# Final scaling in six pieces, extra sums on the Pool engine, and all low halves on DVE

## The chip, the cores and the metric

The kernel runs on one core of one Trainium2 chip, in float32 from end to end. The metric is the device time of one execution in microseconds, as the median of several runs. A profile of one such execution shows every instruction of the five engines: PE (TensorE, with its weight loads as PEld), DVE (VectorE), ACT (ScalarE), POOL (GpSimd) and SP (SyncE, which issues most DMAs).

## The reference, cut to what matters

One decoder layer over 256 tokens: a SwiGLU feed-forward block, a mixer, a second SwiGLU block, and a last RMS norm. The change lies in the second block and in the last norm.

```python
def rmsnorm(x, g):
    y = x32 * lax.rsqrt(jnp.mean(x32 * x32, axis=-1, keepdims=True) + EPS) * g
def swiglu(x, w_gate, w_up, w_down):
    return (jax.nn.silu(x @ w_gate) * (x @ w_up)) @ w_down
h = h + 0.5 * swiglu(rmsnorm(h, ffn2_norm[l]), ffn2_w_gate[l], ffn2_w_up[l], ffn2_w_down[l])
return rmsnorm(h, final_norm)
```

D_MODEL is 2048 and D_FF is 5504. The 256 tokens lie on 128 partitions in two blocks, tb = 0 and 1.

## The kernel before, in words

**A product in three passes.** To keep float32 accuracy, each operand is split into a high half and a low half, and each product is made of three matmuls (`mm3`, lines 95 to 97): high by high, high by low, low by high. The activations' halves (xh, xl) are made once and kept; the weights' halves are made as they stream in. `product` (line 99) walks along the contraction in steps of 4 blocks of 128 rows: `wraw` (line 69) loads 4 blocks by one DMA on the SP queue, then `halves` (line 83) splits them, two blocks at a time, into tiles `whi` and `wlo` of 128x1024. ACT writes `whi` (line 89), and one subtraction writes `wlo` (line 90), as a rule on DVE. Twelve matmuls (two blocks, two token blocks, three passes) consume such a pair. I call it a half and count the halves of the down product's first column chunk from 0 to 21. `whi` and `wlo` have four buffers each, `wraw` three, so ACT and DVE work at most four halves ahead of PE.

**The feed-forward block.** `ffn` (line 295) makes gate and up products for 11 column chunks. DVE then turns each chunk's result with 32 small transposes (line 170, in `turn_split`), which stand in DVE's queue between the subtractions, and `gT` collects 11 pairs of halves. Then come four down products (c = 0 to 3), each 43 blocks deep and 512 columns wide, that is 22 halves, and after each `finish(c)`: in the second block that is `last_chunk` (line 981). It squares and sums h on ACT for the last norm and, for c under 3, multiplies h by its gain (`gfin`, loaded in the call for c = 0 by the ACT queue, line 987). In the product for c = 1 four of the low halves are subtracted on POOL instead of DVE (argument `pooled`, lines 90, 118 and 326).

**The end.** The product for c = 3 holds back the last blocks of token block 1 (`tail`), so that token block 0 finishes some 4 us earlier. For each token block `ffn2` then makes the norm's factor r (lines 968 on DVE and 969 on POOL) and scales the four column chunks: chunk 3 on DVE (line 974, with the gain), chunk 1 on DVE (line 976), chunks 0 and 2 on ACT (line 978), each followed by its output DMA (line 979), from SP for odd chunks and from ACT for even ones.

**What sets the order.** A planner puts each engine's instructions into a queue at build time. It takes what is ready first, as well as the order of the source; each engine then works its queue strictly in order and waits on semaphores. Tiles of up to 4 KB per partition share a ring of 32 slots (`slot`, line 57): a new tile waits until the last reader of its slot's previous tile is done.

Of the kernel before, what the change touches and what calls it, by code (L numbers as in the profile page):

```python
# [9 lines left out]
F32 = mybir.dt.float32  # L10
# [6 lines left out]
P = 128  # L17
D_MODEL = 2048
SEQ = 256
D_FF = 5504  # L20
# [11 lines left out]
class Layer:  # L32
# [47 lines left out]
            k += m  # L80
        return raw

    def halves(self, raw, pool=False):

        nc = self.nc
        _, nk, n = raw.shape
        hi = self.wpool.tile([P, 2, 512], F32R, tag="whi", bufs=4, name=self.name("whi"))
        lo = self.wpool.tile([P, 2, 512], F32R, tag="wlo", bufs=4, name=self.name("wlo"))
        nc.scalar.activation(hi[:, :nk, :n], raw, AF.Copy)  # L89
        (nc.gpsimd if pool else nc.vector).tensor_sub(lo[:, :nk, :n], raw, hi[:, :nk, :n].bitcast(F32))  # L90
        return hi, lo

    def mm3(self, out, xh, xl, wh, wl, first, last):
# [2 lines left out]
        nc.tensor.matmul(out, xh, wl, start=False, stop=False)  # L96
        nc.tensor.matmul(out, xl, wh, start=False, stop=last)  # L97

    def product(self, accs, xT, w, r0, nkt, c0, n, tail=0, pooled=()):


        held = []
        for k0 in range(0, nkt, 4):
            nk = min(4, nkt - k0)
            opening = self.fetch is not None and self.xraw is not None and k0 == 0
            raw = self.wraw(w, r0 + k0 * P, nk, c0, n, (1, 1, 2) if opening else (4,))
            if self.fetch is not None:
                self.fetch(k0 // 4 + 1)
            while any(x is xT[k0 // 4] for x, _ in self.turns):
                self.turns.popleft()[1]()  # L110
            xh, xl = xT[k0 // 4]
            for kk, ke in ((0, 1), (1, 2), (2, 4)) if opening else ((0, 2), (2, 4)):
                ke = min(ke, nk)
                if kk >= ke:
                    continue
                if self.fetch is not None:
                    self.split_x(k0 + kk, k0 + ke)
                wh, wl = self.halves(raw[:, kk:ke, :n], k0 in pooled and kk == 2)
                for k in range(kk, ke):
                    for tb in range(NTB):  # L120
                        ts = slice(tb * P, (tb + 1) * P)
                        mm = partial(
                            self.mm3, accs[tb][:, :n], xh[:, k, ts], xl[:, k, ts], wh[:, k - kk, :n],
                            wl[:, k - kk, :n], k0 + k == 0, k0 + k == nkt - 1,
                        )
                        if tb and k0 + 4 * tail >= nkt:
                            held.append(mm)
                        else:
                            mm()
                while self.soon and k0 + kk >= 2:  # L130
                    self.soon.popleft()()
                for _ in range(min(3, len(self.turns))):
                    self.turns.popleft()[1]()
                self.step()
        for mm in held:
            mm()
# [158 lines left out]
    def ffn(self, wg, wu, wd, finish, tail=0):  # L295
        nc = self.nc
        gT = []
        for c0, n in FCH:
            G = [self.acc("g") for _ in range(NTB)]
            with self.tc.manual_schedule() if self.fetch is not None else nullcontext():  # L300
                self.product(G, self.xT, wg, 0, 16, c0, n)
            self.xraw = None
            U = [self.acc("u") for _ in range(NTB)]
            self.product(U, self.xT, wu, 0, 16, c0, n)
            if self.fetch is not None:
                self.fetch = None
                self.norms()
            pair = self.pair()
            gT.append(pair)
            src = [self.tmp([P, 512], "silu", 2) for _ in range(NTB)]  # L310
            for tb, s in enumerate(src):
                nc.scalar.activation(s[:, :n], G[tb][:, :n], AF.Silu, scale=self.r[tb])
                nc.vector.scalar_tensor_tensor(
                    s[:, :n], U[tb][:, :n], self.r[tb], s[:, :n], op0=ALU.mult, op1=ALU.mult
                )
            if self.later:
                for tb, s in enumerate(src):
                    self.soon.append(partial(self.transpose_split, pair, s, tb, n // P))
            else:
                self.turn_split(pair, src, n // P)  # L320
        self.xT = [None] * 4
        self.st = self.stat(4)
        for c in range(4):
            Y = [self.acc("y") for _ in range(NTB)]
            self.product(Y, gT, wd, 0, D_FF // P, c * 512, 512, tail if c == 3 else 0,
                         (8, 16, 24, 32) if tail and c == 1 else ())
            for tb in range(NTB):
                hs = self.h[:, tb, c * 512 : (c + 1) * 512]
                nc.vector.scalar_tensor_tensor(hs, Y[tb], 0.5, hs, op0=ALU.mult, op1=ALU.add)
            finish(c)  # L330
# [219 lines left out]
    def ssm_groups(self):  # L550
# [3 lines left out]
        for ct in range(8):  # L554
# [14 lines left out]
            def powered(mre, mim, k0, signs):  # L569


                tt = self.slot([P, 4, 256], s="tt")

                def product(t, power, m):
                    for r in range(2):
                        bs = slice(4 * ct + 2 * r, 4 * ct + 2 * r + 2)
                        v.tensor_mul(
                            tt[:, t, r * P : (r + 1) * P].rearrange("s (j x h) -> s x j h", j=4, x=2),
                            self.pw[:, power, k0 : k0 + 4, bs].rearrange("s k b -> s b k").unsqueeze(3)
                            .to_broadcast([P, 2, 4, 16]),  # L580
                            m[:, 2 * r : 2 * r + 2].unsqueeze(2).to_broadcast([P, 2, 4, 16]),
                        )

                product(0, 0, mre)
                product(1, 1, mim)
                v.tensor_tensor(tt[:, 0], tt[:, 0], tt[:, 1], op=signs[0])
                yield tt
                product(2, 0, mim)
                product(3, 1, mre)
                v.tensor_tensor(tt[:, 2], tt[:, 2], tt[:, 3], op=signs[1])  # L590
                yield tt
# [369 lines left out]
    def ffn2(self):  # L961
        t, nc = self.t, self.nc
        self.gfin = None
        self.ffn(t["ffn2_w_gate"][0], t["ffn2_w_up"][0], t["ffn2_w_down"][0], self.last_chunk, 2)
        out = self.out
        for tb in range(NTB):
            r = self.tmp([P, 1], "rstd", 6)
            nc.vector.tensor_scalar(r, self.st[tb][:, 3:4], 1.0 / D_MODEL, self.part[tb], op0=ALU.mult, op1=ALU.add)
            nc.gpsimd.tensor_tensor(r, r, self.mhalf, op=ALU.pow)
            for c in (3, 0, 1, 2):  # L970
                cs = slice(c * 512, (c + 1) * 512)
                hs = self.h[:, tb, cs]
                if c == 3:
                    nc.vector.scalar_tensor_tensor(hs, hs, r, self.gfin[c], op0=ALU.mult, op1=ALU.mult)
                elif c == 1:
                    nc.vector.tensor_scalar(hs, hs, r, None, op0=ALU.mult)
                else:
                    nc.scalar.activation(hs, hs, AF.Copy, scale=r)
                (nc.sync if c % 2 else nc.scalar).dma_start(out[tb, :, cs], hs)

    def last_chunk(self, c):
        nc = self.nc
        if self.gfin is None:
            gf = self.t["final_norm"].rearrange("(o d) -> o d", o=1)
            self.gfin = [self.slot([P, 512], s="gfin") for _ in range(4)]
            for i in range(4):
                nc.scalar.dma_start(
                    self.gfin[i], gf[:, i * 512 : (i + 1) * 512].broadcast_to([P, 512])
                )
        for tb in range(NTB):  # L990
            hs = self.h[:, tb, c * 512 : (c + 1) * 512]
            self.square(self.st[tb], c, hs, 512)
            if c < 3:
                nc.vector.tensor_mul(hs, hs, self.gfin[c])
        if c == 2:
            self.part = []
            for tb in range(NTB):
                p = self.tmp([P, 1], "rstd", 6)
                nc.vector.tensor_reduce(p, self.st[tb][:, :3], axis=mybir.AxisListType.X, op=ALU.add)
                nc.vector.tensor_scalar(p, p, 1.0 / D_MODEL, EPS, op0=ALU.mult, op1=ALU.add)  # L1000
                self.part.append(p)
# [67 lines left out]
```

## Time and profile before

| What | us |
|---|---|
| median of 3 runs | 1809.5 |
| lowest and highest run | 1808.77 and 1809.67 |
| the profiled execution's own time | 1809.42 |
| span of its profile | 1807.6 |
| PE busy within the span | 1792.1 |
| DVE, ACT and POOL busy | 1174.1, 859.3 and 99.9 |

The span is what the engines' records cover; 1.8 us of the execution lie outside it. A line of the timeline reads: start and length in us, engine and line of the kernel, operation, output <- inputs, shape, count, and in brackets the idle time before it and what ended it. Times within the span count from its start.

### The profile page before, as it was taken

The numbers are of one execution on the slowest core, as the hardware profiler recorded it, in microseconds if no ns is written. First come the engines' busy times: TensorE is split into PE (matmuls) and PEld (weight loads), VectorE is DVE, ScalarE is ACT, GpSimd is POOL, SyncE is SP. The second block draws the span as 40 slices with busy tenths as digits, with TensorE's granted clock in tenths as the row PEclk, the third lists the DMA queues.
The fourth block names the chain that finished last, engine by engine and source line by source line (L and its number), as shares of the span: only waits on it lengthen the run. The fifth ranks groups of instructions, "written<-read, shape, count | busy, mean of one in ns | idle before, by whom it ended". The sixth has DMA issues, their size and how long they took to land.

```text
span 1807.6 us, 22050 instructions
## 1 busy us (share of the span) xinstructions
PE 1792.1 (99%) x8365; PEld 1502.2 (83%) x8365; DVE 1174.1 (65%) x2024; ACT 859.3 (48%) x1190; POOL 99.9 (6%) x177
## 2 busy tenths in 40 slices
PE   8999999999999999999999999999999999999997
PEld 6888888788988888888888888888888888988886
DVE  5796588777765545566766565776777777853453
ACT  6544567444444434443358555444444444443443
POOL 2102022500000000000000000000000000002000
PEclk9999999999999999999999999999999999999999
DMA  8667667865555557676443455556556555665553
GB/s 321 198 218 242 202 233 255 266 218 181 190 191 201 181 192 267 202 272 239 155 147 133 140 186 186 187 192 201 189 189 201 192 187 163 212 224 191 199 197 117
DMA packets 180330, 364.18 MB, mean 201 GB/s; under 512 B 8256, under 2 KB 17344, under 8 KB 179968
## 3 DMA queue, kind: packets, MB, share of 16 engines
q1 hardware_dynamic: 172192, 343.96, 56.7%
q0 software_dynamic: 6736, 16.69, 2.7%
q10 hardware_dynamic: 1296, 2.13, 0.4%
q8 instruction: 65, 1.06, 0.2%
q14 instruction: 41, 0.34, 0.1%
HBM read 346.36 MB, written 16.38 MB: 201 GB/s over the span
## 4 chain that ended last, share of the span: by engine, by line
PE 93%; DVE 3%; DMA 1%; issue 1%; ACT 1%; POOL 0%; SPq 0%; POOLq 0%; ACTq 0%
PE y L96 9%; PE y L95 9%; PE y L97 9%; PE u L96 8%; PE u L97 8%; PE u L95 8%; PE g L96 7%; PE g L97 7%; PE g L95 7%; PE pr L95 3%; PE pr L97 3%; PE pr L96 3%; PE wo L95 2%; PE wo L97 2%; PE wo L96 2%; DVE turned L170 1%
## 5 line engine op out<-in xcount | busy, mean ns | idle before, releaser
L90 DVE TENSOR_TENSOR wlo<-wraw,whi 128x1024 fp32r<-128x1024 f32 (+2 forms) x629 | 752.1, 1201 | 551.2 <-ACT whi L89 548.4
L89 ACT ACTIVATE whi<-wraw 128x1024 fp32r<-128x1024 f32 (+2 forms) x633 | 657.2, 1042 | 771.5 <-PE y L97 247.3
L95 PE MATMUL g<-whi,xh 128*128 128x512 f32 (+1 forms) x704 | 271.7, 386 | 2.2 <-ACT whi L89 2.1
L96 PE MATMUL g<-wlo,xh 128*128 128x512 f32 (+1 forms) x704 | 271.1, 385 | 2.6 <-DVE wlo L90 2.6
L96 PE MATMUL u<-wlo,xh 128*128 128x512 f32 (+1 forms) x704 | 270.8, 385 | 0.1
L95 PE MATMUL u<-whi,xh 128*128 128x512 f32 (+1 forms) x704 | 270.8, 385 | 0.0
L97 PE MATMUL g<-whi,xl 128*128 128x512 f32 (+1 forms) x704 | 270.6, 384 | 0.0
L97 PE MATMUL u<-whi,xl 128*128 128x512 f32 (+1 forms) x704 | 270.4, 384 | 0.0
L95 PE MATMUL y<-whi,xh 128*128 128x512 f32 x688 | 267.9, 389 | 0.0
L97 PE MATMUL y<-whi,xl 128*128 128x512 f32 x688 | 267.7, 389 | 0.0
L96 PE MATMUL y<-wlo,xh 128*128 128x512 f32 x688 | 267.7, 389 | 0.0
L170 DVE STREAM_TRANSPOSE turned<-silu 32x128 f32<-32x128 f32 (+1 forms) x512 | 152.8, 298 | 8.1
L96 PEld LDWEIGHTS g<-wlo,xh 128*128 128x128 f32 x704 | 132.2, 188 | 29.3 <-DVE wlo L90 4.7
L95 PEld LDWEIGHTS g<-whi,xh 128*128 128x128 f32 x704 | 132.2, 188 | 28.2 <-ACT whi L89 3.5
L96 PEld LDWEIGHTS u<-wlo,xh 128*128 128x128 f32 x704 | 132.1, 188 | 26.0 <-DVE wlo L90 1.1
L97 PEld LDWEIGHTS u<-whi,xl 128*128 128x128 f32 x704 | 132.1, 188 | 25.0
L97 PEld LDWEIGHTS g<-whi,xl 128*128 128x128 f32 x704 | 132.1, 188 | 24.9
L95 PEld LDWEIGHTS u<-whi,xh 128*128 128x128 f32 x704 | 132.1, 188 | 24.8
L97 PEld LDWEIGHTS y<-whi,xl 128*128 128x128 f32 x688 | 129.1, 188 | 26.9
L95 PEld LDWEIGHTS y<-whi,xh 128*128 128x128 f32 x688 | 129.1, 188 | 26.8
L96 PEld LDWEIGHTS y<-wlo,xh 128*128 128x128 f32 x688 | 129.1, 188 | 26.6
L95 PE MATMUL pr<-whi,xh 128*128 128x512 f32 x256 | 101.9, 398 | 0.0
(212 smaller groups left out, 1515.7 us busy)
## 6 DMA issues: line engine op xcount, KB each, us to landing
wraw<-in_ffn_w_up SPq DMA_DIRECT2D x80, 1024.0 KB, 5.1
wraw<-in_ffn_w_down SPq DMA_DIRECT2D x80, 1024.0 KB, 5.1
wraw<-in_ffn_w_gate SPq DMA_DIRECT2D x79, 1024.0 KB, 5.1
wraw<-in_w_in SPq DMA_DIRECT2D x32, 1024.0 KB, 5.4
wraw<-in_w_out SPq DMA_DIRECT2D x16, 1024.0 KB, 5.1
wraw<-in_ffn_w_gate SPq DMA_DIRECT2D x8, 768.0 KB, 4.5
wraw<-in_ffn_w_up SPq DMA_DIRECT2D x8, 768.0 KB, 4.5
wraw<-in_ffn_w_down SPq DMA_DIRECT2D x8, 768.0 KB, 4.4
```

What stands on the lines that cost most here:

```text
L89: nc.scalar.activation(hi[:, :nk, :n], raw, AF.Copy)
L90: (nc.gpsimd if pool else nc.vector).tensor_sub(lo[:, :nk, :n], raw, hi[:, :nk, :n].bitcast(F32))
L95: nc.tensor.matmul(out, xh, wh, start=first, stop=False)
L96: nc.tensor.matmul(out, xh, wl, start=False, stop=False)
L97: nc.tensor.matmul(out, xl, wh, start=False, stop=last)
L170: nc.vector.transpose(raw[32 * b : 32 * b + 32, :nt, tb * P + 32 * a : tb * P + 32 * a + 32], src[tb][32 * a : 32 * a + 32, : nt * P].rear ...
```

## The change

The diff does three things. It takes the `pooled` choice away, so that every low half is subtracted on DVE. It adds, in the call of `last_chunk` for c = 0, three slot tiles of 128x1024, two memsets and sixteen equal additions of two of them into the third on POOL, whose result nobody reads. And at the end it scales in the order chunk 1 (DVE), two parts of chunk 0 (ACT), chunk 3 (DVE), two parts of chunk 2 (ACT), with all six output DMAs of a token block issued by SP.

```diff
-    def halves(self, raw, pool=False):
+    def halves(self, raw):
...
-        (nc.gpsimd if pool else nc.vector).tensor_sub(lo[:, :nk, :n], raw, hi[:, :nk, :n].bitcast(F32))
+        nc.vector.tensor_sub(lo[:, :nk, :n], raw, hi[:, :nk, :n].bitcast(F32))
...
-                wh, wl = self.halves(raw[:, kk:ke, :n], k0 in pooled and kk == 2)
+                wh, wl = self.halves(raw[:, kk:ke, :n])
...
-            self.product(Y, gT, wd, 0, D_FF // P, c * 512, 512, tail if c == 3 else 0,
-                         (8, 16, 24, 32) if tail and c == 1 else ())
+            self.product(Y, gT, wd, 0, D_FF // P, c * 512, 512, tail if c == 3 else 0)
...
-            for c in (3, 0, 1, 2):
-                cs = slice(c * 512, (c + 1) * 512)
+            pieces = ((1, 0, 512), (0, 0, 256), (0, 256, 512), (3, 0, 512), (2, 0, 256), (2, 256, 512))
+            for c, lo, up in pieces:
+                cs = slice(c * 512 + lo, c * 512 + up)
...
-                (nc.sync if c % 2 else nc.scalar).dma_start(out[tb, :, cs], hs)
+                nc.sync.dma_start(out[tb, :, cs], hs)
...
+        if c == 0:
+
+            z = [self.slot([P, 1024], s="z") for _ in range(3)]
+            for x in z[:2]:
+                nc.gpsimd.memset(x, 0.0)
+            for _ in range(16):
+                nc.gpsimd.tensor_add(z[2], z[0], z[1])
```

## Rows read from the trace of the kernel before

**Rows 1.** The page, parts 1 and 4: busy time by engine, and the chain by engine.

```profile
PE 1792.1 (99%) x8365; PEld 1502.2 (83%) x8365; DVE 1174.1 (65%) x2024; ACT 859.3 (48%) x1190; POOL 99.9 (6%) x177
...
PE 93%; DVE 3%; DMA 1%; issue 1%; ACT 1%; POOL 0%; SPq 0%; POOLq 0%; ACTq 0%
```

**Rows 2.** Busy time by stage: stretch, its length, busy us (and instructions) by engine, PE clock, DMA.

```profile
1565.00:1585.00 20.00, 20.00 (x89) 16.52 (x89) 18.88 (x43) 8.66 (x9) 0.00 (x0) 1.00 0.59 199
1622.00:1681.00 59.00, 59.00 (x262) 48.87 (x261) 23.94 (x23) 24.78 (x27) 9.60 (x4) 1.00 0.56 192
```

**Rows 3.** Timeline of PE: first matmuls of the last up product and the first down product.

```profile
1547.23 0.34 PE L95 MATMUL u<-whi,xh 128*128 128x384 f32 x1
...
1564.35 0.39 PE L95 MATMUL y<-whi,xh 128*128 128x512 f32 x1
```

**Rows 4.** Timeline of DVE across the start of the first down product, 1561 to 1600.

```profile
1561.48 1.23 DVE L90 TENSOR_TENSOR wlo<-wraw,whi 128x1024 fp32r<-128x1024 f32 x1 [0.85 <-ACT whi L89]
...
1565.24 0.61 DVE L313 SCALAR_TENSOR_TENSOR silu<-u,rstd,silu 128x384 f32<-128x384 f32 x1
1565.76 2.52 DVE L170 STREAM_TRANSPOSE turned<-silu 32x96 f32<-32x96 f32 x9
1568.31 1.23 DVE L90 TENSOR_TENSOR wlo<-wraw,whi 128x1024 fp32r<-128x1024 f32 x1
...
1574.96 2.81 DVE L170 STREAM_TRANSPOSE turned<-silu 32x96 f32<-32x96 f32 x10
1577.80 1.23 DVE L90 TENSOR_TENSOR wlo<-wraw,whi 128x1024 fp32r<-128x1024 f32 x1
...
1581.08 0.95 DVE L177 TENSOR_TENSOR xl<-turned,xh 128x768 fp32r<-128x768 f32 x1
...
1595.61 1.23 DVE L90 TENSOR_TENSOR wlo<-wraw,whi 128x1024 fp32r<-128x1024 f32 x1 [1.49 <-ACT whi L89]
```

**Rows 5.** Timeline of POOL from 1300 on: the first of its four subtractions.

```profile
1629.65 2.39 POOL L90 TENSOR_TENSOR wlo<-wraw,whi 128x1024 fp32r<-128x1024 f32 x1 [530.67 <-ACT whi L89]
```

**Rows 6.** Timeline of ACT and its DMA issues: the gain loads of line 987.

```profile
1579.93 0.85 ACT L176 ACTIVATE xh<-turned 128x768 fp32r<-128x768 f32 x1 [3.40 <-DVE turned L170]
1579.94 0.82 ACTq L987 DMA_DIRECT2D gfin<-in_final_norm  x2
```

**Rows 7.** POOL's instructions by line: memsets of 128x1024.

```profile
L597 POOL MEMSET C<- x8: 972/976/987, 153.0 to 305.4; 128x1024 f32 x8
```

**Rows 8.** Timelines of DVE and POOL at 972, and of POOL at 42.

```profile
972.06 1.22 DVE L90 TENSOR_TENSOR wlo<-wraw,whi 128x1024 fp32r<-128x1024 f32 x1
...
972.22 1.46 POOL L199 TENSOR_TENSOR rstd<-rstd,even 128x1 f32<-128x1 f32 x1 [2.83 <-DVE rstd L198]
...
42.47 1.09 POOL L199 TENSOR_TENSOR rstd<-rstd,even 128x1 f32<-128x1 f32 x2 [29.70 <-DVE rstd L198]
```

**Rows 9.** Timeline of the end: scaling and output DMAs of token block 1.

```profile
1800.87 1.33 ACT L978 ACTIVATE h<-h,rstd 128x512 f32<-128x512 f32 x2 [0.91 <-POOL rstd L969]
1800.87 0.75 DVE L974 SCALAR_TENSOR_TENSOR h<-h,rstd,gfin 128x512 f32<-128x512 f32 x1 [0.67 <-POOL rstd L969]
1801.54 0.48 DVE L976 TENSOR_SCALAR h<-h,rstd 128x512 f32<-128x512 f32 x1
1801.62 0.95 ACTq L979 DMA_DIRECT2D out<-h  x2
```

**Rows 10.** Issues of the output DMAs on SP: ns shortest/median/longest.

```profile
L979 SPq DMA_DIRECT2D out<-h x4: 332/367/448, 1796.9 to 1802.1; - x4
```

**Rows 11.** Busy time in stretches of 1 us at the end; columns as in rows 2.

```profile
1799.00:1800.00 1.00, 0.00 (x0) 0.00 (x0) 0.21 (x2) 0.72 (x2) 0.00 (x0) 1.00 1.01 385
...
1802.00:1803.00 1.00, 0.00 (x0) 0.00 (x0) 0.02 (x1) 0.21 (x1) 0.00 (x0) 0.50 0.51 197
...
1804.00:1805.00 1.00, 0.00 (x0) 0.00 (x0) 0.00 (x0) 0.00 (x0) 0.00 (x0) 0.50 1.03 383
1805.00:1806.00 1.00, 0.00 (x0) 0.00 (x0) 0.00 (x0) 0.00 (x0) 0.00 (x0) 0.50 0.30 107
```

More of the change, by code (lines that the diff above doesn't have):

```diff
@@ L97, in mm3, with product @@
         nc.tensor.matmul(out, xl, wh, start=False, stop=last)
-    def product(self, accs, xT, w, r0, nkt, c0, n, tail=0, pooled=()):
+    def product(self, accs, xT, w, r0, nkt, c0, n, tail=0):
         held = []
```

## The prediction, made before the changed kernel was run

> **What bounds the kernel now.** I read the chain of waits first: PE makes 93% of it, POOL nothing, and POOL is busy 6% of the span [rows 1]. The busy time by stage then says how much room the other engines have. In the second down product (c = 1, 59 us) PE is full and DVE works 23.94 us; in the 20 us at the start of the first one PE is also full, but DVE works 18.88 us [rows 2]. So nothing that DVE or ACT does costs time as long as PE's next low half is there, and the one place where this could fail soon is 1565 to 1585, where the 32 small transposes stand between the subtractions in DVE's queue.
>
> How much room there is, the two timelines tell together. PE starts the first down product at 1564.35 [rows 3] and spends 2.72 us on a half (in steady state a subtraction every 1.23 + 1.49 us, paced by PE [rows 4]). Half n therefore starts at 1564.35 + 2.72n, and its low half is wanted 0.23 us later (a twelfth of 2.72), at the second matmul. Half 6 is wanted at 1580.9; its subtraction is the one at 1577.80, done at 1579.03 [rows 4]: 1.9 us to spare. In steady state it is more: the buffer is freed three halves (8.16 us) ahead and ACT and DVE need some 2.6 us of that, which leaves about 5.5 us.
>
> **The low halves back on DVE.** Four subtractions of 2.39 us leave POOL [rows 5] and four of 1.23 us [rows 4] come to DVE: 4.9 us in a stage where DVE idles 35 of 59 us [rows 2]. The idle time hides them; PE doesn't wait there now. Price 0, and none without that cover either, since 1.23 us is sooner than 2.39.
>
> **The sums: where they run.** The source puts them after the first down product, but POOL's queue holds nothing that keeps them there: POOL idles 530.67 us up to its first subtraction at 1629.65 [rows 5]. The gain loads of the same call show how far such work is pulled ahead: they are issued at 1579.94, some 42 us before that product ends at 1564.35 + 21 x 2.72 + 1.36 = 1622.8, and stand behind an ACT instruction that waited 3.40 us [rows 6]. On POOL only the slots can hold the sums. Of 32 slots gT keeps 22 and the gains take 4, so three of the remaining six serve: those of the second block's x halves, which come free one after the other while the last up product (1547.23 to 1564.35 [rows 3]) reads them. The gains come first and take the earliest ones. My estimate: the second memset starts when three quarters of that product are done, 1560.1, takes 0.98 us [rows 7], and the first addition starts at 1561.1. The bounds are 1556 and 1582.0, the end of the last split at L177 [rows 4].
>
> **The sums: what one costs.** No row has such an addition; the nearest is POOL's subtraction of the same shape, with two SBUF inputs too: 2.39 us [rows 5]. All four stood beside an idle DVE. What happens beside a working one shows in one place: the small power on POOL takes 0.55 us when it is alone (1.09 for two), and took 1.46 us where it started at 972.22, 0.16 us behind a DVE subtraction (972.06 to 973.28); it ended 0.40 us after that one [rows 8]. So it had 0.15 us of its start behind it, and then stood still until DVE was done: POOL's reads and a DVE subtraction exclude each other. That DVE stands still for POOL in the same way no row shows. I take it to be mutual. An addition then holds DVE's subtractions for 2.39 - 0.15 = 2.25 us; the bounds are 2.0 (if all but the 0.15 us of the power's 0.55 is a fixed cost free of reads, 2.39 - 0.40) and 2.4.
>
> [...]
>
> **The sum.** If the two engines take turns, one addition, one subtraction, a turn takes 2.25 + 1.23 = 3.48 us, against the 2.72 us in which PE eats a half. In two places two additions run with no subtraction between them: under the last product's scaling and the 9 transposes (to 1568.31) and under the 10 transposes (2.81 us) [rows 4]. The 16 additions then hold 14 DVE instructions between and behind them: halves 1 to 13 and the split at L177. The last is done at 1561.1 + 16 x 2.25 + 13 x 1.23 + 0.95 = 1614.0. PE wants half 13 at 1564.35 + 13 x 2.72 + 0.23 = 1599.9: 14.1 us late. After that DVE is quick again, and nothing is won back, since PE has no slack to win. With 2.0 us per addition it is 10.1, with 2.4 16.5; a handing over of 0.1 us per turn would add 1.4. The starting point counts little, because an earlier or later start meets the same turns: from 1582, 16 additions and the subtractions of halves 8 to 23 (half 21 a short one, some 0.7 us) end at 1637.2, where half 23 is wanted at 1622.8 + 2.72 + 0.23 = 1625.8, so 11.4 us.
>
> PE would pause for up to some 3 us at a time. [...]
>
> **The end.** After the last matmul the chain runs through the norm's factor to ACT's scaling, the output DMAs, and their transfer: 1 MB from 1802.5 (share 0.51 of that microsecond) to 1805.3 (share 0.30) at about 383 GB/s [rows 11]. Before, the first piece is out at 1801.62 (DVE's 0.75 us from 1800.87, and ACT's first issue then) [rows 9]. With chunk 1 first, DVE needs 0.48 us: 1801.35, so the stream starts 0.27 us sooner. Six issues on SP at 0.33 to 0.45 us [rows 10] put the last one at 1801.4 + 5 x 0.45 = 1803.6 at the latest; ACT's four parts, by 1.33 us for two wholes [rows 9] between 1.33 and 2.67 us in all, end by 1803.5 too. From issue to data is 0.9 us and 128 KB take 0.34 us: 1804.9, while the bus alone needs until 1802.2 + 2.75 = 1805.0. So -0.3 us; bounds -0.4 and +0.6, the latter if the issues and parts take their longest and don't overlap. SP has no other work left there; ACT loses two issues. The same DMAs of token block 0 lie 4 us earlier, beside matmuls.
>
> Forecast: 1809.42 + 14.1 - 0.3 = 1823.2 us for an execution like the profiled one; the median lies 0.1 above it, so 1823. Own range 1819 to 1830 (2.0 us per addition; 2.4 with handing over and 3 us of clock).
>
> **Rivals.** [...]
>
> Second, POOL doesn't let go between additions. DVE's half 1 (1561.48 [rows 4]) then waits for all sixteen, 1561.1 + 38.2 = 1599.3, and PE, which wants it at 1567.3, is 33 us late at least; the transposes that pile up add some 2: 1845. Against it: the pair of powers took exactly twice one [rows 8], so a start of some 0.15 us or more lies between POOL's instructions. [...]
>
> Third, on the other side: only POOL gives way, and DVE's subtractions never wait, or for under 0.3 us each, which the 1.9 us to spare absorbs over the seven halves at the start. Then the sums are free and only the end counts: 1809.1. For it: the one row that shows the conflict has POOL as the loser. It decides as soon as a subtraction's wait for an addition stays below that 0.3 us.
>
> [...]
>
> **How the numbers follow.** Forecast 0.42, first rival 0.20, second 0.08, third 0.28, something else 0.02. A measurement of this kernel tells about 0.2% (3.6 us) from no change. The third rival is "same", as is the lower third of the first (0.06, up to 1813.1); the second and the rest of the first are slower: slower 0.64, same 0.34, faster 0.02. The range takes in the third rival, the first and the forecast: 1808.5 to 1830; it leaves out the second.
>
> **What would show it.** POOL's 16 additions from about 1561, each of 2.4 to 3.7 us in the record; DVE's subtractions there longer than 1.23 us or starting late, with POOL named as what they wait for or an unexplained gap; PE idle at `wlo` between 1573 and 1615 for 14 us in all; the spacing of PE's halves near 3.5 us in that stretch. [...] Six SP issues per token block and a transfer that ends 0.3 us sooner behind the last matmul would bear out the end. What would make me wrong most easily is the direction of the wait.

## The result and the profile after

The changed kernel takes 1822.37 us (median of 6 runs, 1820.31 to 1823.99) against 1809.68 us for the kernel before (6 runs): a ratio of 1.007, 95% interval 1.006 to 1.0081. It is 12.7 us slower; the forecast was 1823. The profiled execution took 1823.05 us, its span is 1821.2 us. One execution below, of the kernel without the sums, took 2589.65 us at a mean granted clock of 0.652; the ratios leave it out.

The page of the changed kernel, parts 1 and 4, answers to [rows 1]:

```profile
PE 1798.3 (99%) x8365; PEld 1504.7 (83%) x8365; DVE 1203.2 (66%) x2028; ACT 860.1 (47%) x1194; POOL 141.3 (8%) x191
...
PE 75%; DVE 5%; issue 2%; ACT 1%; DMA 1%; POOL 0%; POOLq 0%; ACTq 0%
```

POOL is 41 us busier, yet the chain still gives POOL nothing: what it costs shows under other names. Here is POOL's timeline, from 1300 on, for the changed kernel (start, length, engine, line, operation, count, idle time before):

```profile
1557.00 0.95 POOL L994 MEMSET z<- 128x1024 f32 x1 [457.30 <-PE u L97]
1561.03 0.95 POOL L994 MEMSET z<- 128x1024 f32 x1 [3.08 <-ACT whi L89]
1562.07 50.38 POOL L996 TENSOR_TENSOR z<-z,z 128x1024 f32<-128x1024 f32 x16
```

Its first two additions by themselves:

```profile
1562.07 2.40 POOL L996 TENSOR_TENSOR z<-z,z 128x1024 f32<-128x1024 f32 x1
1564.54 3.26 POOL L996 TENSOR_TENSOR z<-z,z 128x1024 f32<-128x1024 f32 x1
```

The sums begin at 1562.07, before the product that they follow in the source has begun. The first addition, ahead of DVE, takes 2.40 us; the sixteen last 50.38 us. Beside them runs DVE (its timeline; it answers to [rows 4]):

```profile
1562.22 3.32 DVE L90 TENSOR_TENSOR wlo<-wraw,whi 128x1024 fp32r<-128x1024 f32 x1 [0.85 <-ACT whi L89]
...
1565.47 3.42 DVE L90 TENSOR_TENSOR wlo<-wraw,whi 128x1024 fp32r<-128x1024 f32 x1
...
1569.86 2.51 DVE L170 STREAM_TRANSPOSE turned<-silu 32x96 f32<-32x96 f32 x9
1572.41 2.29 DVE L90 TENSOR_TENSOR wlo<-wraw,whi 128x1024 fp32r<-128x1024 f32 x1
...
1581.41 2.81 DVE L170 STREAM_TRANSPOSE turned<-silu 32x96 f32<-32x96 f32 x10
1584.25 2.89 DVE L90 TENSOR_TENSOR wlo<-wraw,whi 128x1024 fp32r<-128x1024 f32 x1
...
1590.38 3.15 DVE L177 TENSOR_TENSOR xl<-turned,xh 128x768 fp32r<-128x768 f32 x1
...
1596.77 3.39 DVE L90 TENSOR_TENSOR wlo<-wraw,whi 128x1024 fp32r<-128x1024 f32 x1
...
1600.09 3.42 DVE L90 TENSOR_TENSOR wlo<-wraw,whi 128x1024 fp32r<-128x1024 f32 x1
...
1610.12 3.41 DVE L90 TENSOR_TENSOR wlo<-wraw,whi 128x1024 fp32r<-128x1024 f32 x1
...
1617.50 1.23 DVE L90 TENSOR_TENSOR wlo<-wraw,whi 128x1024 fp32r<-128x1024 f32 x1 [0.57 <-ACT whi L89]
```

None of the slow subtractions has idle time before it but the first, and its 0.85 us are those of the kernel before: each is recorded as a busy instruction of up to 3.4 us, though it takes 1.23 us when nothing stands in its way. In this record a blocked instruction looks like a slow one. The transposes, which have one SBUF input, take what they took before (2.51 us for nine against 2.52, 2.81 for ten in both kernels). And this is what reached PE: all the waits of its matmuls between 1555 and 1660, in the timeline of PE:

```profile
1574.76 0.50 PE L96 MATMUL y<-wlo,xh 128*128 128x512 f32 x1 [1.07 <-DVE wlo L90]
1578.09 0.50 PE L96 MATMUL y<-wlo,xh 128*128 128x512 f32 x1 [0.32 <-DVE wlo L90]
1581.43 0.50 PE L96 MATMUL y<-wlo,xh 128*128 128x512 f32 x1 [0.31 <-DVE wlo L90]
1587.20 0.69 PE L96 MATMUL y<-wlo,xh 128*128 128x512 f32 x1 [2.75 <-DVE wlo L90]
1596.90 0.50 PE L96 MATMUL y<-wlo,xh 128*128 128x512 f32 x1 [2.37 <-DVE wlo L90]
1610.25 0.50 PE L96 MATMUL y<-wlo,xh 128*128 128x512 f32 x1 [0.33 <-DVE wlo L90]
1613.58 0.50 PE L96 MATMUL y<-wlo,xh 128*128 128x512 f32 x1 [0.32 <-DVE wlo L90]
```

They sum to 7.5 us only, where the prediction looked for 14. The starts of the matmuls, 0.227 us apart in the kernel before, tell where the rest lies: the pauses in front of a low half put them back by 8.7 us, two stretches under a slow clock by 3.3 us more, and the steps right behind the pauses by about 1 us. Time under a slow clock counts as busy (from 1588 to 1590 PE is busy all 2 us, at a granted clock of 0.50; more below), so a busy PE of 99% hides it. A better measure is the length of a product. I take the first down product from its first matmul to DVE's first addition to h behind it (line 329, now 328):

```profile
1565.09 0.39 PE L95 MATMUL y<-whi,xh 128*128 128x512 f32 x1
...
1636.13 0.69 DVE L328 SCALAR_TENSOR_TENSOR h<-y,h 128x512 f32<-128x512 f32 x1 [1.08 <-PE y L97]
```

That is 71.04 us, against 58.04 before (1564.35 to 1622.39): 13.00 us more. From there to the last such addition it is 176.12 us in both kernels. So the whole loss lies in the first down product. What is left of the difference of the two spans (13.6 us) is 0.74 us ahead of 1565, where the eleven profiles of this study scatter from 1562.2 to 1565.9, and -0.14 us behind the last addition.

### The profile page after: what moved, and what is told of

It reads as the page before. It is cut to its first block, busy times and chain, and to the rows that moved or that the text cites. A ratio compares the mean times of both kernels' runs of the same rounds, so it can differ in the third digit from the quotient of the medians.

```text
span 1821.2 us, 22082 instructions
## 1 busy us (share of the span) xinstructions
PE 1798.3 (99%) x8365; PEld 1504.7 (83%) x8365; DVE 1203.2 (66%) x2028; ACT 860.1 (47%) x1194; POOL 141.3 (8%) x191
## 3 DMA queue, kind: packets, MB, share of 16 engines
q10 hardware_dynamic: 720, 1.08, 0.2%
## 4 chain that ended last, share of the span: by engine, by line
PE 75%; DVE 5%; issue 2%; ACT 1%; DMA 1%; POOL 0%; POOLq 0%; ACTq 0%
PE y L96 8%; PE y L95 8%; PE y L97 8%; PE u L96 6%; PE u L97 6%; PE u L95 6%; PE g L96 5%; PE g L97 5%; PE g L95 5%; PE pr L95 3%; PE pr L97 3%; PE pr L96 3%; DVE wlo L90 3%; DVE turned L170 2%; PE wo L95 2%
## 5 line engine op out<-in xcount | busy, mean ns | idle before, releaser
L90 DVE TENSOR_TENSOR wlo<-wraw,whi 128x1024 fp32r<-128x1024 f32 (+2 forms) x633 | 779.1, 1237 | 535.1 <-ACT whi L89 532.1
```

The source lines that it names most:

```text
L90: nc.vector.tensor_sub(lo[:, :nk, :n], raw, hi[:, :nk, :n].bitcast(F32))
```

## The experiments

The theory: POOL's reads and DVE's two-input subtractions exclude each other and take turns, and a turn (one POOL instruction and one subtraction) is longer than the time in which PE uses up a half. The rivals are other parts of the change, other properties of POOL's work, and other ways to count the price. Below, product lengths are as just defined; product c = 1 runs from there to the next such addition (58.48 us before).

**Without the sums.** Taken out:

```diff
-        if c == 0:
...
-            for _ in range(16):
-                nc.gpsimd.tensor_add(z[2], z[0], z[1])
```

> The changed kernel with the two memsets and sixteen additions taken out; the low halves all on DVE and the six-piece scaling stay. Theory (the sums' turns with DVE's subtractions are the whole loss): 1809.2 to 1809.7, that is the time of before less 0.1 to 0.3 us, PE without idle time in the first down product, DVE's subtractions at 1.23 us. Rival (part of the loss comes from the four low halves moved to DVE or from the output DMAs all on SP): over 1813.

Measured: 1809.95 us, ratio 1.0001 (0.9992 to 1.0011). First product 58.04 us, DVE's subtractions 1.23 us. The low halves on DVE and the DMAs on SP cost nothing that shows.

**The sums alone.** The kernel before with the same block added, nothing else changed:

```diff
+        if c == 0:
...
+            for _ in range(16):
+                nc.gpsimd.tensor_add(z[2], z[0], z[1])
```

> The kernel before with the memsets and sixteen additions alone; four low halves on POOL and the old scaling stay. Theory: 1822.5, like the changed kernel to within 1.5 us, POOL's additions 3.26 us each from about 1562. Rival (the loss needs the other edits too): below 1817.

Measured: 1821.77 us, ratio 1.0066 (1.0051 to 1.0081); first product 71.07 us, additions 3.26 us each. The sums are the loss, by themselves. What in them?

**POOL busy, but not reading.**

```diff
-            for _ in range(16):
-                nc.gpsimd.tensor_add(z[2], z[0], z[1])
+            for _ in range(40):
+                nc.gpsimd.memset(z[2], 0.0)
```

> The changed kernel with forty memsets of 128x1024 in place of the sixteen additions: about as long on POOL (40 x 0.95 = 38 us), in the same place, but POOL only writes SBUF and reads nothing. Theory (what shuts DVE out is that POOL reads SBUF while a DVE instruction with two SBUF inputs wants to): no loss, 1809.2 to 1809.7, memsets at 0.95 us, subtractions at 1.23. Rival (any POOL work in SBUF shuts DVE's subtractions out, or the three extra slot tiles delay something): memsets and subtractions take turns of 1.23 + 0.95 us; there are 40 of them, and the loss is over 4 us.

Measured: 1809.05 us, ratio 0.9996 (0.9987 to 1.0006), first product 58.04 us. The instructions on the tile z (POOL) and on wlo (DVE, 1562 to 1616) in this kernel, ns shortest/median/longest:

```profile
L996 POOL MEMSET z<- x40: 952/956/959, 1561.3 to 1600.8; 128x1024 f32 x40
...
L90 DVE TENSOR_TENSOR wlo<-wraw,whi x21: 694/1226/1226, 1561.6 to 1614.3; 128x1024 fp32r<-128x1024 f32 x20, 128x512 fp32r<-128x512 f32 x1
```

Forty us of writing in the same place, and neither engine feels the other. It is neither POOL's work as such nor the three slots, but its reads.

**One input instead of two.**

```diff
-            for _ in range(16):
-                nc.gpsimd.tensor_add(z[2], z[0], z[1])
+            for _ in range(32):
+                nc.gpsimd.tensor_copy(z[2], z[0])
```

> The changed kernel with 32 copies of 128x1024 (one SBUF input each) in place of the 16 additions (two). It asks whether one input is enough to shut out DVE's subtractions. Theory (any POOL read of SBUF does): subtractions of 1.8 us and more beside the copies, copies longer than alone; if a copy takes about 1.1 us, a turn takes under 2.72 us, so the time stays within 3 us of before. Rival (only a two-input instruction does): subtractions at 1.23 us throughout.

Measured: 1808.78 us, ratio 0.9997 (0.9986 to 1.0007), first product 58.04 us. The same view of this kernel, wlo from 1562 to 1600:

```profile
L996 POOL COPY z<-z x32: 1039/1914/2094, 1559.0 to 1612.0; 128x1024 f32<-128x1024 f32 x32
...
L90 DVE TENSOR_TENSOR wlo<-wraw,whi x15: 1224/1852/2057, 1561.4 to 1598.9; 128x1024 fp32r<-128x1024 f32 x15
```

One input is enough: copies go from 1.04 to 1.91 us, subtractions from 1.23 to 1.85 (medians). But a turn of some 2 us (seven subtractions in a row, from 1581.77, take 13.92) is shorter than PE's 2.72, so nothing is lost.

**The same elements in half-size additions.**

```diff
-            for _ in range(16):
-                nc.gpsimd.tensor_add(z[2], z[0], z[1])
+            for i in range(32):
+                s = slice(i % 2 * 512, i % 2 * 512 + 512)
+                nc.gpsimd.tensor_add(z[2][:, s], z[0][:, s], z[1][:, s])
```

> The changed kernel with 32 additions of 128x512 in place of 16 of 128x1024: the same elements, half as many per instruction. Theory (a turn of one addition and one subtraction is compared with the 2.72 us that PE spends on a half): an addition holds DVE for some 1.0 to 1.1 us, a turn takes 2.2 to 2.4 us, less than 2.72, so PE loses only what the crowded stretch at the start costs: 1810 to 1813. [...]

Measured: 1810.58 us, ratio 1.0008 (0.9998 to 1.0017); first product 59.42 us, 1.38 us more than before instead of 13.00. The same view of this kernel:

```profile
L997 POOL TENSOR_TENSOR z<-z,z x32: 1281/2268/2281, 1561.8 to 1622.4; 128x512 f32<-128x512 f32 x32
...
L90 DVE TENSOR_TENSOR wlo<-wraw,whi x20: 1226/2304/2317, 1562.0 to 1613.8; 128x1024 fp32r<-128x1024 f32 x20
```

POOL is busy longer than in the changed kernel (to 1624 instead of 1612), and more of DVE's instructions are held up (23 take longer than alone, against 14). What counts is the single turn: some 2.23 us, under 2.72. The one wait of PE's matmuls, 0.65 us at 1588.13, comes at the end of the stretch that the transposes crowd.

**The price of a further addition.**

```diff
-            for _ in range(16):
+            for _ in range(24):
                 nc.gpsimd.tensor_add(z[2], z[0], z[1])
```

> The changed kernel with 24 additions in place of 16. In the changed kernel a turn takes 3.34 us and PE has no slack left by the sixteenth. Theory (a further addition costs the turn less PE's 2.72 us for a half): 8 x 0.62 = 5.0 us more than the changed kernel, about 1827.4. Rivals: the average price goes on (13.0 us for 16, 0.81 each): 6.5 us more, 1828.9; each addition costs its whole hold of 2.1 us: 17 us more, 1839.

Measured: 1826.48 us, ratio 1.0096 (1.0081 to 1.0111). The first two down products together take 133.93 us (129.52 in the changed kernel): 4.4 us more for eight additions, 0.55 each; by the medians it is 4.1. Nearest is the turn less PE's half (5.0); the average price (6.5) is further off, the whole hold (17) is out. The 0.6 us that are missing lie in the last turn, which holds the short half 21 (DVE's timeline):

```profile
1635.78 2.87 DVE L90 TENSOR_TENSOR wlo<-wraw,whi 128x512 fp32r<-128x512 f32 x1
```

It ends 2.80 us after the subtraction before it instead of 3.34, so that turn costs 0.1 us: 7 x 0.62 + 0.1 = 4.4.

**The sums inside a quiet product.**

```diff
+        if c == 0:
+            z = [self.slot([P, 2, 512], s="z") for _ in range(2)]
+            nc.gpsimd.memset(z[0], 0.0)
+            for _ in range(16):
+                nc.gpsimd.tensor_add(z[1], z[0], self.h[:, :, :512])
```

written after the loop that multiplies h by the gain, in place of the block ahead of it.

> The changed kernel with the sixteen additions tied to the end of the first down product: they read h's first column chunk as second input and are written after its gain multiplication, so that they run inside the second down product, where DVE has no transposes and idles 1.49 us per half. Theory: the same turns of 3.34 us, but some 5.5 us of lead to use up first: 16 x (3.34 - 2.72) - 5.5 = 4.4 us, 1814; the step of the prediction that said the place changes little if they take turns (11.4 us) used the lead at half 8, not that of the steady state. Rival (DVE wins each contest while it is behind): 1809.5. Rival (the place counts for nothing): 1822.

Measured: 1814.34 us, ratio 1.0028 (1.0017 to 1.0039). POOL's and DVE's timelines of this kernel, and the end of product c = 1:

```profile
1629.02 53.28 POOL L999 TENSOR_TENSOR z<-z,h 128x1024 f32<-128x1024 f32 x16 [70.23 <-DVE h L994]
...
1633.91 2.70 DVE L90 TENSOR_TENSOR wlo<-wraw,whi 128x1024 fp32r<-128x1024 f32 x1 [0.65 <-ACT whi L89]
1636.63 3.30 DVE L90 TENSOR_TENSOR wlo<-wraw,whi 128x1024 fp32r<-128x1024 f32 x1
...
1663.27 3.42 DVE L90 TENSOR_TENSOR wlo<-wraw,whi 128x1024 fp32r<-128x1024 f32 x1
...
1686.95 0.69 DVE L328 SCALAR_TENSOR_TENSOR h<-y,h 128x512 f32<-128x512 f32 x1 [0.69 <-PE y L97]
```

Product c = 0 is back at 58.04 us, and c = 1 takes 62.98: 4.50 us more, where 4.4 was worked out. The same sixteen additions, the same turns, a third of the loss.

**Few enough to hide.**

```diff
-            for _ in range(16):
+            for _ in range(8):
                 nc.gpsimd.tensor_add(z[1], z[0], self.h[:, :, :512])
```

> The kernel with the sums tied to the end of the first down product, with 8 additions in place of 16 (16 of them cost 4.9 us by the median). Theory (a turn of 3.34 us loses 0.62 us per half, and the lead of some 5.5 us is used up first): 8 x 0.62 = 5.0 us is less than the lead, so no loss, 1809.2 to 1810.0, and no idle time of PE at the low halves of the second down product. Rival (each addition costs its share, 0.31 us): 1811.9.

Measured: 1809.92 us, ratio 0.9994 (0.9985 to 1.0003); both products at 58.04 and 58.48 us, no wait of PE. DVE's subtractions still reach 3.43 us there. The loss isn't proportional: eight additions cost nothing that shows and sixteen 4.50 us, so there is a lead to use up, and up to it the blocking is free here.

**The end, with the order alone.**

```diff
-            pieces = ((1, 0, 512), (0, 0, 256), (0, 256, 512), (3, 0, 512), (2, 0, 256), (2, 256, 512))
+            pieces = ((1, 0, 512), (0, 0, 512), (3, 0, 512), (2, 0, 512))
...
-                nc.sync.dma_start(out[tb, :, cs], hs)
+                (nc.sync if c % 2 else nc.scalar).dma_start(out[tb, :, cs], hs)
```

> No sums, low halves all on DVE, and the scaling in four whole pieces in the order chunk 1, 0, 3, 2 with the DMAs on SP for odd and ACT for even chunks. It tells the order's part of the end from that of the six pieces on one queue. Theory: from DVE's last addition to h to the end of the span before 9.09 us, changed 8.95 us; here 8.8, because the first piece is out 0.27 us sooner and whole pieces move at 383 GB/s, not at the 312 to 315 of the halves. Rival (pieces and queue make no difference, only the order): 8.95. The time itself, 1809.2 to 1809.6, will not tell them apart.

Measured: 1808.97 us, ratio 0.9998 (0.9989 to 1.0008); from the last addition to h to the end of the span 9.12 us, not 8.8. A miss. Over the profiles of this study that stretch is 8.89 to 9.21 us with six pieces (eight kernels, mean 9.00) and 8.93 and 9.09 with the old end. None of the three ends can be told from the others.

No kernel here beats the one before: the five with nothing blocking long enough (without sums, memsets, copies, eight additions later, four pieces) lie within 0.1% of it.

## Why the prediction was right

The stated range, 1808.5 to 1830, is wide enough to hold the time of before as well, so it is the steps below that bear the forecast out, not the range. That the profiled execution (1823.05) lies within 0.2 us of the 1823.2 forecast for one like it is partly luck: the product cost 1.1 us less than forecast, and 0.74 us came from a later start.

**What bounds the kernel.** Right: PE, and the crowded stretch (1565 to 1585) as the place where it could fail. PE's first wait for a low half is at half 3 (1574.76), the longest at half 6 (1587.20).

**The low halves on DVE.** Right: product c = 1 takes 58.48 us in both kernels.

**Where the sums run.** Right, and read off the gain loads [rows 6] and POOL's idle queue [rows 5]: first memset at 1557.00, second at 1561.03, first addition at 1562.07, where 1561.1 was estimated (and this execution was 0.74 us late by then).

**What an addition costs.** The mechanism was right: the exclusion is mutual. An addition beside a subtraction takes 3.26 us where the first took 2.40, and the subtraction at 1565.47 takes 3.42 where one alone takes 1.23. Of this [rows 8] show POOL's side only, in one blocked power. That DVE waits too, the step that carried the forecast and was the least certain, was the author's assumption; no run before this one shows it. Nor does one show that additions run on beside the scaling and the transposes, as the count of 14 has it; here the addition at 1571.22, beside transposes, takes 2.39 us, and the one at 1583.71 takes 2.35. The price was a little high: a turn takes 3.34 us (1596.77 to 1600.09 is 3.32; 1600.09 to 1610.12, three turns, 10.03), not 3.48. Counted with the whole 1.23 us of a subtraction the hold is 2.11 us, between the bounds 2.0 and 2.4 and below the chosen 2.25 (2.39 - 0.15 is 2.24). But POOL's part was right: the second addition ends at 1567.80, 2.26 us behind the subtraction that it waited for (1565.54). The term that was too big is DVE's: a subtraction ends 3.34 - 2.26 = 1.08 us behind the addition, not 1.23. DVE too has some 0.15 us of its start behind it when its turn comes, which the prediction granted to POOL alone.

**The sum.** Fourteen DVE instructions stand between and behind the sixteen additions, and half 13 is the last late one, as counted: its subtraction starts at 1610.12 and ends at 1613.53. PE wanted it at 1565.09 + 13 x 2.72 + 0.23 = 1600.7; 12.8 us late, and 13.00 by the product's length, against 14.1 forecast. From the first addition to that end it is 51.5 us instead of 52.9: DVE's fourteen instructions take 2.0 us less, and 0.6 of that was lost again, mostly in the three additions that have no subtraction in front of them to cover POOL's start (the first, and the second of each pair in a row). And the first addition began 3.0 us ahead of PE's first matmul, not 3.25.

**The clock.** No run shows the 3 us of clock in the upper end of the range; that was the author's estimate. The granted clock did fall, from 1.00 to 0.50, and put the matmuls back by the 3.3 us above, but that added nothing to the loss. Two stretches of the changed kernel (length, busy us by engine, granted clock, DMA share); each begins or ends at full speed, so its clock is a mean:

```profile
1587.00:1589.00 2.00, 1.80 (x5) 1.43 (x6) 1.91 (x5) 0.95 (x2) 2.00 (x1) 0.59 0.00 0
1589.00:1591.00 2.00, 2.00 (x7) 1.59 (x6) 2.00 (x2) 1.79 (x2) 1.92 (x2) 0.56 0.59 219
```

After a pause from 1584.4 to 1587.2 PE worked at a granted clock of 0.50 until 1590.7, its matmuls 0.43 us apart instead of 0.23, and again after the next long pause (1597.5 to 1600.8). Each time it had caught up with DVE before it waited for the next low half (2.37 us at 1596.90, and 0.32 us as late as 1613.58), and DVE itself was never idle from 1562.22 to 1616.93. So the slow stretches came out of time that PE would have waited anyway. The forecast, which added nothing for the clock, held.

**The end.** Wrong in size: -0.3 us was forecast, and nothing can be shown. The stream does start sooner (3.8 us behind the last addition to h instead of 4.0), but it moves more slowly. The last microseconds of the changed kernel, which answer to [rows 11]:

```profile
1815.00:1816.00 1.00, 0.00 (x0) 0.00 (x0) 0.81 (x2) 1.00 (x4) 0.00 (x0) 1.00 0.00 0
1816.00:1817.00 1.00, 0.00 (x0) 0.00 (x0) 0.00 (x0) 0.37 (x1) 0.00 (x0) 0.52 0.99 359
1817.00:1818.00 1.00, 0.00 (x0) 0.00 (x0) 0.00 (x0) 0.00 (x0) 0.00 (x0) 0.50 1.09 314
1818.00:1819.00 1.00, 0.00 (x0) 0.00 (x0) 0.00 (x0) 0.00 (x0) 0.00 (x0) 0.50 1.03 312
1819.00:1820.00 1.00, 0.00 (x0) 0.00 (x0) 0.00 (x0) 0.00 (x0) 0.00 (x0) 0.50 0.26 71
```

The DMA engines are as busy as before and move 312 to 359 GB/s instead of 371 to 385, so the step that failed is the one that took 383 GB/s for the new stream as well. That the parts of 128 KB are the reason isn't shown. With whole pieces in the new order, on two queues, the full stretches of half a microsecond moved 311 to 369 GB/s; the slowest of them:

```profile
1804.80:1805.30 0.50, 0.00 (x0) 0.00 (x0) 0.00 (x0) 0.00 (x0) 0.00 (x0) 0.50 1.12 311
```

Nor was the time to the end of the span shorter there. Why the rate falls stays open, and 0.2 us is below what separates kernels with the same end (8.89 to 9.21 us).

**The rivals.** The first (DVE wins while it is behind) falls with the first contested hand-over: the subtraction of half 2 is ready as that of half 1 ends (1565.54; its `whi` was done at 1564.27), and yet takes 3.42 us, because POOL, whose second addition had waited since 1564.54, went first. The second (POOL doesn't let go) falls with the turns. The third (only POOL gives way) falls with every subtraction of 3.4 us.

**The step that was wrong, without harm.** The prediction said that the starting point counts little. It counts much: 13.0 us where the transposes crowd DVE, 4.5 us in the quiet product. The 11.4 us worked out for a start at 1582 had a lead of only 1.6 us in it, since the crowd had eaten the rest, turns of 3.48 us, and the short half 21 in the way. With the 5.5 us of the steady state and turns of 3.34 us the working gives 4.4, and 4.50 was measured. No run has the sums in the middle of the first product itself.

## What to carry to other kernels

Here POOL's additions and copies, which read SBUF, and DVE's instructions with two SBUF inputs excluded each other and took turns (an addition 3.26 us instead of 2.40, a subtraction 3.4 instead of 1.23, the split at L177 3.15 instead of 0.95), so the idle POOL wasn't free room; price such work by one turn (the POOL instruction's hold plus DVE's own time) against the time in which the bounding engine uses up what DVE made, less the lead of the buffers. If the turn is longer, cut the POOL instructions in half or use fewer of them: the same elements cost 13.0 us in pieces of 1024 and 1.4 us in pieces of 512. And look where independent work really runs: POOL's queue had nothing in front of the sums, and they started at 1562.07, 3.0 us ahead of the product that they follow in the source, in the busiest 20 us of the neighbour [rows 2].

## What the runs showed of the hardware that was not expected

- The turns are strict. With both queues full an addition and a subtraction alternate every 3.34 us (three turns from 1600.09 take 10.03), and the instruction that was already waiting goes ahead of the next one of the engine that has just finished (the addition that waited from 1564.54 ahead of the subtraction at 1565.47); the record of each (3.26 and 3.4 us) includes its wait for the other, so neither shows idle time.
- One SBUF input on POOL was enough to block (copies: 1.04 us the shortest, 1.91 the median, beside subtractions of 1.85 instead of 1.23), none wasn't (memsets: 0.95 us throughout, subtractions 1.23), and DVE's one-input transposes weren't touched (2.51 us for nine, 2.81 for ten).
- The products repeat to within 0.01 us from profile to profile (58.04 and 58.48 us in every undisturbed one), while whole runs scatter by several us: in the eleven profiles the scatter lies ahead of the second block's down products, which start between 1562.2 and 1565.9. A stretch of the trace resolved what the medians couldn't.
